# A gate's condition blocks multiplied and added by GpSimd instead of VectorE

## The chip, the cores and the metric

One core of one Trainium2 chip runs the whole kernel in one launch. The metric is the device time of one execution in microseconds (us). Engines are named as the profile names them: PE is TensorE (matmuls), PEld its weight loads, DVE is VectorE, ACT is ScalarE, POOL is GpSimd, SP is SyncE. Each engine works through its own queue in order.

## The reference

A trunk of four layers over 512 tokens of width 1024, in float32. Each layer has a token mixer (latent attention, stick-breaking attention, retention, latent attention) and a dense MLP. Each half layer is normed, shifted and scaled ahead of the mixer or MLP, and gated behind it, by vectors that come from one condition vector:

```
cond = silu(c)                                   # (1, 1024)
mod = cond @ ada_w[i] + ada_b[i]                 # (1, 6144), for layer i
sh_a, sc_a, g_a, sh_f, sc_f, g_f = split(mod, 6)
h = rms_norm(x, norm_g[i, 0]) * (1 + sc_a) + sh_a
x = x + g_a * rms_norm(mixer(h), norm_g[i, 1])
h = rms_norm(x, norm_g[i, 2]) * (1 + sc_f) + sh_f
x = x + g_f * rms_norm(mlp(h), norm_g[i, 3])
```

The latent attention of layers 0 and 3 has 8 heads with a causal softmax over 512 keys. The change touches `g_a` of layer 0, the gate that is applied to the attention's output.

## The kernel before, in words

Float32 products on PE are made of three passes over a high and a low part of each operand (`mm3`, lines 91 to 93); `split` (lines 85 and 86) makes the parts, the high one on ACT, the low one on DVE. Tokens are worked in four blocks of 128.

**The condition products.** A vector such as `g_a` is 1024 columns of `cond @ ada_w`. The first shift and scale are made at the start (`ada_start`); all others are made by the generator `ada`, beside other work. Its rows are cut into eight blocks of 128 rows, 512 KB each. For a block, `load` issues a DMA in POOL's queue (line 301) into a raw tile 128x1024, of which there are three. DVE then multiplies the tile by the block's 128 condition values, one per partition (line 313, the first block, into the accumulator `adaacc`), or multiplies and adds to the accumulator in one instruction (line 315, the seven others). So partition p of `adaacc` holds the sum of eight rows, and what is left is a sum over partitions: `columns_of` does that by DVE transposes of 32x32 (line 338), DVE sums (line 341), a matmul with a folding matrix (line 348) and small additions. A call of `next(bg)` makes one block, or one step of `columns_of`. A load is issued two blocks ahead, and waits for its raw tile to be free.

**The work around it.** During layer 0's attention `bg` is `ada` with the gate's job first (blocks 0 to 7) and then shift and scale of the MLP half (blocks 8 to 23). The attention is a pipeline over heads; at each step t the program text has, in this order:

```
order = ((B, 0), (C1, 1), (C2, 2), (A, -2), (B2, 0))   # stage, lag
for stage, lag in order:
    if 0 <= t - lag < n:
        stage(t - lag)
if t >= 0:
    for _ in range(3):
        next(bg, None)
```

`A` makes k, q and, for every fourth head, v of a head (PE, with copies on ACT and DVE; lines 751 to 758 rotate q). `B` is `softmax_rows`: the scores on PE; on DVE a mask and a row maximum per query block (line 884); on POOL one instruction on a 128x4 tile that turns the maxima into biases (line 887); on ACT the exponentials with their sums (line 889). `B2` takes reciprocals of the sums on DVE (line 783) and normalises on ACT (line 785). `C1` transposes the probabilities on PE (line 903) and splits them, `C2` multiplies with v. The banks of PSUM that these stages use are shared, four for the scores and four for all else.

**Who sets the order.** A planner puts every engine's instructions into a queue ahead of time: it plays the program through with its own durations, and each engine takes, of what is ready, what stands first in the program text. `held` and `after` add order without a wait. The queues are then fixed. At the start of the kernel (lines shown as L1305) instructions go strictly in the text's order.

Later stages (the attention's output projection, where the gate is first used, the MLP and the other layers) follow in PE's queue.

Of the kernel before, what the change touches and what calls it, by code (L numbers as in the profile page):

```python
# [12 lines left out]
ALU = mybir.AluOpType  # L13

P = 128
S = 512
# [27 lines left out]
class Trunk:  # L44
# [239 lines left out]
            pass  # L284
        yield

    def ada(self, jobs):

        nc = self.nc
        blocks = [(job, i, kb) for job in jobs for i in range(len(job[2])) for kb in range(KB)]
        raws, due, sums = {}, [], {}

        def load(n):
            if n < len(blocks):
                (l, part, names), i, kb = blocks[n]
                col = (3 * part + self.ROWS[names[i]]) * D
                raws[n] = self.adap.tile([P, D], F32, tag="araw", name="adaraw", bufs=AHEAD + 1)  # L300
                self.after(nc.gpsimd.dma_start(out=raws[n], in_=self.d_ada_w[l][kb * P:kb * P + P, col:col + D]), self.mm)  # L301

        for n in range(AHEAD):
            load(n)
        for n, (job, i, kb) in enumerate(blocks):
            load(n + AHEAD)
            if due and next(due[0], self) is self:
                due.pop(0)
            rv = raws.pop(n)
            wcol = self.cond[:, kb:kb + 1]  # L310
            if kb == 0:
                a = self.adap.tile([P, D], F32, tag="acc", name="adaacc", bufs=1)
                ins = nc.vector.tensor_scalar(a, rv, wcol, None, ALU.mult)
            else:
                ins = nc.vector.scalar_tensor_tensor(a, rv, wcol, a, ALU.mult, ALU.add)  # L315
            self.held(ins)
            if kb == KB - 1:
                due.append(self.columns_of(job, i, a, sums))
            yield
        while due:  # L320
            if next(due[0], self) is self:
                due.pop(0)
            else:
                yield
# [892 lines left out]
    def run(self, ctx):  # L1217
        nc = self.nc
        mixers = self.mixers
        kinds = {"mla": self.mla, "sb": self.sb, "ret": self.ret}  # L1220
        none = lambda: None
        tables = {"mla": (lambda: list(self.mla_tables()), self.mla_tables_T), "sb": (none, none), "ret": (self.ret_tables, none)}
        self.xn, self.mods, self.gates = {}, {}, {}
        self.hold = self.late = None
        phases = []
        seen = {}
        bg = self.ada([(0, 0, ("G",)), (0, 1, ("sh", "S"))])
        for l, kind in enumerate(mixers):
            j = seen[kind] = seen.get(kind, -1) + 1
            m, f = Phase(l, 0), Phase(l, 1)  # L1230
            wanted = [(0, 1, ("G",))] if l == 0 else []
            if l + 1 < len(mixers):
                wanted += [(l + 1, p, ("sh", "S", "G")) for p in (0, 1)]
                t = tables[mixers[l + 1]]
            else:
                t = (none, none)
            m.gen = lambda nxt, k=kinds[kind], j=j, m=m, bg=bg: k(j, m, nxt, bg)
            f.gen = lambda nxt, l=l, f=f, bg=self.ada(wanted), t=t: self.ffn(l, f, nxt, bg, t)
            bg = iter(())
            phases += [m, f]  # L1240
        for a, b in zip(phases, phases[1:] + [None]):
            a.nxt = b
        first, mod = phases[0], (0, 0)
        self.starting, self.h_pool = True, True
        setup = self.setup(ctx)
        next(setup)
        halves = [self.ada_start([(n, half) for n in ("S", "sh")]) for half in (0, 1)]
        rope = self.mla_tables()
        next(halves[0])
        for _ in setup:  # L1250
            pass
        next(rope)
        for _ in range(X0 - 1):
            next(halves[0])
        self.load_x()
        next(halves[0])
        next(rope)
        rs = [self.x_rstd(tb) for tb in range(TB)]
        for tb in range(TB):
            self.pre_norm(tb, rs[tb])  # L1260
        next(rope)
        for _ in range(7 - X0):
            next(halves[0])
        first.go()
        for _ in halves[0]:
            pass
        for _ in rope:
            pass
        for _ in range(ST0):
            next(halves[1])  # L1270
        for g in (0, 1):
            for kb in (0, 2):
                self.turn(g, mod, kb, kb + 2)
                for _ in range(ST1):
                    next(halves[1], None)
        for _ in range(8 - ST0 - 4 * ST1):
            next(halves[1])
        first.go()
        for _ in halves[1]:
            pass  # L1280
        first.go()
        self.h_pool = False
        for g in (0, 1):
            self.turn(g, mod, 4, 8)
        tables[mixers[0]][1]()
        self.starting = False
        for p in phases:
            p.finish()
# [94 lines left out]
```

## Time and profile before

| what | value |
|---|---|
| median of 3 runs | 2502.9 us (2502.72 to 2504.25) |
| the profiled execution's own time | 2503.81 us |
| its span in the trace | 2502.0 us |
| mean granted clock of PE | 0.991 |
| PE busy | 2418.3 us, 97% |
| DVE busy | 1544.3 us, 62% |
| ACT busy | 1089.1 us, 44% |
| POOL busy | 248.5 us, 10% |
| layer 0's attention heads (about) | 84 to 180 us |
| the gate's eight blocks on DVE | 94.2 to 112.3 us |

The span is what lies between the first and the last instruction in the trace; the execution's time is 1.8 us longer. Busy shares are of the whole span: what an engine's time is worth in one stage is read from that stage.

### The profile page before, as it was taken

Reading aid. Unit: us, or ns where it says so; the run is one execution under the profiler, and the core shown is the slowest. Engines: PE = TensorE matmul, PEld = TensorE weight load, DVE = VectorE, ACT = ScalarE, POOL = GpSimd, SP = SyncE. Lnnn points to the kernel's source line nnn. Section 1 sums busy time; section 2 is a strip of 40 time slices with the busy share of each in tenths; the row PEclk is TensorE's granted clock in tenths of the full one; section 3 lists DMA queues with packets and bytes.
Section 4 is the critical chain, followed back from the end, with each engine's and each line's share of the span. In section 5 each row is a group of like instructions: output and inputs, shape, how many; then the busy total and the mean of one; then the engine's idle time right before and its main releaser. Section 6 shows DMA issues by size and latency. Waiting matters only on the chain.

```text
span 2502.0 us, 30936 instructions
## 1 busy us (share of the span) xinstructions
PE 2418.3 (97%) x11733; PEld 2027.1 (81%) x11733; DVE 1544.3 (62%) x2333; ACT 1089.1 (44%) x2002; POOL 248.5 (10%) x495
## 2 busy tenths in 40 slices
PE   5889999999998999999999999999999999999998
PEld 4778888888886888888788888888888778888886
DVE  6896666666888567765644444476665676633443
ACT  6665332235665533323533334453233576632331
POOL 5311100101000110000100000100010310000000
PEclk9999999999999999999999999999999999999999
DMA  7354765743210475663322232365663303333331
GB/s 237 99 177 137 236 200 173 219 144 125 64 35 25 153 236 157 210 200 99 128 76 92 80 103 85 112 219 166 210 209 95 96 18 127 96 99 101 94 95 48
DMA packets 204534, 329.95 MB, mean 132 GB/s; under 512 B 15968, under 2 KB 115168, under 8 KB 204384
## 3 DMA queue, kind: packets, MB, share of 16 engines
q1 hardware_dynamic: 179040, 235.69, 29.9%
q0 software_dynamic: 25344, 92.29, 11.5%
q8 instruction: 92, 1.51, 0.2%
q14 instruction: 58, 0.48, 0.1%
HBM read 319.51 MB, written 8.42 MB: 131 GB/s over the span
## 4 chain that ended last, share of the span: by engine, by line
PE 84%; DVE 6%; ACT 5%; issue 3%; POOL 2%; DMA 1%; SPq 0%; POOLq 0%; DVEq 0%; ACTq 0%
PE acc L93 15%; PE acc L92 15%; PE acc L91 15%; PE mmp L91 13%; PE mmp L92 13%; PE mmp L93 13%; ACT probs L889 1%; ACT junk L136 1%; POOL rstd L131 1%; PE trp L903 1%; DVE u L1029 1%; POOL var L128 1%; DVE x L439 0%; DVE b L1030 0%; ACT probs L785 0%
## 5 line engine op out<-in xcount | busy, mean ns | idle before, releaser
L86 DVE TENSOR_TENSOR wl<-raw,wh 128x1024 fp32r<-128x1024 f32 (+1 forms) x356 | 434.5, 1223 | 422.6 <-ACT wh L85 420.1
L85 ACT CAST wh<-raw 128x1024 fp32r<-128x1024 f32 (+1 forms) x356 | 373.7, 1051 | 656.0 <-PE acc L93 369.3
L92 PE MATMUL mmp<-hl,wh 128*128 128x512 f32 (+1 forms) x1408 | 520.8, 371 | 2.4 <-DVE hl L86 2.4
L93 PE MATMUL mmp<-hh,wl 128*128 128x512 f32 (+1 forms) x1408 | 519.7, 370 | 0.0
L91 PE MATMUL mmp<-hh,wh 128*128 128x512 f32 (+1 forms) x1408 | 518.5, 372 | 1.0 <-DVE ol L86 0.9
L91 PE MATMUL acc<-wh,h1h 128*128 128x512 f32 x1024 | 399.2, 390 | 0.0
L93 PE MATMUL acc<-wh,h1l 128*128 128x512 f32 x1024 | 398.5, 389 | 0.0
L92 PE MATMUL acc<-wl,h1h 128*128 128x512 f32 x1024 | 398.5, 389 | 0.0
L92 PEld LDWEIGHTS mmp<-hl,wh 128*128 128x128 f32 x1408 | 265.3, 188 | 48.3 <-DVE hl L86 3.9
L93 PEld LDWEIGHTS mmp<-hh,wl 128*128 128x128 f32 x1408 | 265.3, 188 | 45.0
L91 PEld LDWEIGHTS mmp<-hh,wh 128*128 128x128 f32 x1408 | 263.5, 188 | 47.2 <-DVE ol L86 2.0
L93 PEld LDWEIGHTS acc<-wh,h1l 128*128 128x128 f32 x1024 | 192.2, 188 | 39.9
L92 PEld LDWEIGHTS acc<-wl,h1h 128*128 128x128 f32 x1024 | 192.3, 188 | 39.8
L91 PEld LDWEIGHTS acc<-wh,h1h 128*128 128x128 f32 x1024 | 192.2, 188 | 39.9
L315 DVE SCALAR_TENSOR_TENSOR adaacc<-adaraw,cond,adaacc 128x1024 f32<-128x1024 f32 x154 | 197.1, 1280 | 6.0 <-DMA adaraw<-in_ada_w_dram 5.4
L301 POOL DMA_DIRECT2D adaraw<-in_ada_w_dram x176 | 94.1, 535 | 749.4 <-DVE adaacc L315 428.9
L85 ACT CAST h1h<-relu 128x512 fp32r<-128x512 f32 (+1 forms) x144 | 81.8, 574 | 143.0 <-DVE relu L529 143.0
L528 ACT ACTIVATE relu<-mmp 128x512 f32<-128x512 f32 (+1 forms) x144 | 77.9, 547 | 123.4 <-PE mmp L93 123.1
L93 PE MATMUL acc<-wh,hl 128*128 128x512 f32 (+1 forms) x320 | 123.8, 390 | 5.6 <-DVE hl L86 4.3
L529 DVE TENSOR_TENSOR relu<-mmp,relu 128x512 f32<-128x512 f32 (+1 forms) x144 | 89.7, 627 | 62.5 <-ACT relu L528 62.4
L91 PE MATMUL acc<-wh,hh 128*128 128x512 f32 (+1 forms) x320 | 124.2, 391 | 4.1 <-ACT hh L1305 3.8
L86 DVE TENSOR_TENSOR h1l<-relu,h1h 128x512 fp32r<-128x512 f32 (+1 forms) x144 | 90.2, 631 | 59.9 <-ACT h1h L85 59.9
(309 smaller groups left out, 3603.8 us busy)
## 6 DMA issues: line engine op xcount, KB each, us to landing
raw<-in_ffn_w_dram SPq DMA_DIRECT2D x256, 512.0 KB, 3.8
adaraw<-in_ada_w_dram POOLq DMA_DIRECT2D x176, 512.0 KB, 4.8
raw<-in_ret_w_in_dram SPq DMA_DIRECT2D x48, 512.0 KB, 4.0
raw<-in_sb_w_in_dram SPq DMA_DIRECT2D x24, 512.0 KB, 3.8
x<-x SPq DMA_DIRECT2D x48, 256.0 KB, 3.6
adaw<-in_ada_w_dram SPq DMA_DIRECT2D x32, 256.0 KB, 5.3
raw<-in_mla_w_out_dram SPq DMA_DIRECT2D x16, 512.0 KB, 4.5
raw<-in_ret_w_out_dram SPq DMA_DIRECT2D x16, 512.0 KB, 4.4
```

Of the source, the lines that this page charges most:

```text
L85: ins = self.nc.scalar.copy(hi, src)
L86: (engine or self.nc.vector).tensor_sub(lo, src, hi.bitcast(F32))
L91: first = self.mm = mm(ps, l[0], r[0], start=start, stop=False)
L92: mm(ps, l[0], r[1], start=False, stop=False)
L93: mm(ps, l[1], r[0], start=False, stop=stop)
L128: self.nc.gpsimd.tensor_scalar(v, ss, ss2, EPS, ALU.add, ALU.add)
L131: self.last = self.nc.gpsimd.tensor_tensor(r, v, self.mhalf[:, 0:w], ALU.pow)
L136: self.nc.scalar.activation(junk[:, 0:src.shape[-1]], src, AF.Square, scale=scale, accum_out=acc_out)
L301: self.after(nc.gpsimd.dma_start(out=raws[n], in_=self.d_ada_w[l][kb * P:kb * P + P, col:col + D]), self.mm)
L315: ins = nc.vector.scalar_tensor_tensor(a, rv, wcol, a, ALU.mult, ALU.add)
L528: nc.scalar.activation(r, ps, AF.Relu)
L529: nc.vector.tensor_mul(r, ps, r)
```

## The change

The eight blocks of layer 0's first gate go from DVE to POOL. [...] So one multiply and seven multiply-adds on DVE become eight multiplies and seven additions on POOL. Loads, transposes and everything behind them stay on their engines, and all other jobs keep DVE. The POOL instructions aren't `held`.

```
-    def ada(self, jobs):
+    def ada(self, jobs, pool_job=None):
...
             wcol = self.cond[:, kb:kb + 1]
             if kb == 0:
                 a = self.adap.tile([P, D], F32, tag="acc", name="adaacc", bufs=1)
-                ins = nc.vector.tensor_scalar(a, rv, wcol, None, ALU.mult)
+            if job == pool_job:
+                t = a if kb == 0 else rv
+                nc.gpsimd.tensor_scalar(t, rv, wcol, None, ALU.mult)
+                if kb:
+                    nc.gpsimd.tensor_tensor(a, a, rv, ALU.add)
+            elif kb == 0:
+                self.held(nc.vector.tensor_scalar(a, rv, wcol, None, ALU.mult))
             else:
-                ins = nc.vector.scalar_tensor_tensor(a, rv, wcol, a, ALU.mult, ALU.add)
-            self.held(ins)
+                self.held(nc.vector.scalar_tensor_tensor(a, rv, wcol, a, ALU.mult, ALU.add))
...
-        bg = self.ada([(0, 0, ("G",)), (0, 1, ("sh", "S"))])
+        bg = self.ada([(0, 0, ("G",)), (0, 1, ("sh", "S"))], (0, 0, ("G",)))
```

## Rows read from the trace of the kernel before

**Rows 1.** The page: busy us, share of span, instructions of each engine.
```profile
PE 2418.3 (97%) x11733; PEld 2027.1 (81%) x11733; DVE 1544.3 (62%) x2333; ACT 1089.1 (44%) x2002; POOL 248.5 (10%) x495
```

**Rows 2.** By stretches: length, busy PE, PEld, DVE, ACT, POOL; PE clock; DMA.
```profile
100.00:120.00 20.00, 16.27 (x78) 13.45 (x77) 16.75 (x31) 14.33 (x35) 2.95 (x6) 0.91 0.54 171
120.00:140.00 20.00, 18.16 (x99) 15.38 (x98) 19.44 (x44) 11.59 (x32) 3.10 (x7) 0.91 0.33 94
...
180.00:200.00 20.00, 20.00 (x102) 16.63 (x101) 14.78 (x23) 9.43 (x14) 0.00 (x0) 1.00 0.58 187
```

**Rows 3.** Chain of waits, 84 to 130 us: start, length, who.
```profile
89.06 2.30 ACT probs L889 x8
...
94.32 0.67 DVE adaacc L313
...
97.30 4.91 DMA adaraw<-in_ada_w_dram
...
102.30 1.29 DVE adaacc L315
...
104.70 0.40 ACT probs L785
```

**Rows 4.** Timeline of PE: start, length, instruction, idle before and releaser.
```profile
105.15 0.33 PE L903 MATMUL trp<-ident,probs 128*128 128x128 f32 x1 [3.11 <-ACT probs L785]
...
121.55 1.25 PE L903 MATMUL trp<-ident,probs 128*128 128x128 f32 x10
```

**Rows 5.** DVE's instructions by groups, 93 to 125 us.
```profile
L315 DVE SCALAR_TENSOR_TENSOR adaacc<-adaraw,cond,adaacc 128x1024 f32<-128x1024 f32 x7 | 9.0, 1281 | 1.6 <-DMA adaraw<-in_ada_w_dram 1.5
```

**Rows 6.** Timeline of ACT and DVE between 98 and 123 us.
```profile
98.92 0.40 ACT L889 ACTIVATE probs<-probs,max 128x128 f32<-128x128 f32 x1 [2.76 <-POOL max L887]
...
109.73 2.60 DVE L315 SCALAR_TENSOR_TENSOR adaacc<-adaraw,cond,adaacc 128x1024 f32<-128x1024 f32 x2
...
113.61 1.64 ACT L785 ACTIVATE probs<-probs,rz 128x256 f32<-128x256 f32 x3
...
122.51 0.70 DVE L338 STREAM_TRANSPOSE aT<-adaacc 128x512 f32<-128x512 f32 x1
```

**Rows 7.** Timeline of POOL at the start of the kernel.
```profile
1.14 0.29 POOL masks.py:199 TENSOR_SCALAR_AFFINE_SELECT ident<-ident 128x128 f32<-128x128 f32 x1
...
18.28 0.30 POOL L1305 TENSOR_SCALAR var<-ssx 128x1 f32<-128x1 f32 x1 [0.41 <-ACT junk L1305]
...
26.49 0.83 POOL L1305 TENSOR_TENSOR ropet<-ropet 128x128 f32<-128x128 f32 x1 [5.25 <-ACT ropet L1305]
...
29.04 0.55 POOL L1305 TENSOR_SCALAR snk<-ropek 128x128 f32<-128x128 f32 x1
...
36.20 1.18 POOL L1305 TENSOR_TENSOR hl<-ht,hh 128x256 fp32r<-128x256 f32 x1
...
58.20 0.19 POOL L130 TENSOR_SCALAR var<-ssq 128x1 f32<-128x1 f32 x1 [3.18 <-ACT junk L136]
```

**Rows 8.** Timeline of DVE and POOL where the two run at once.
```profile
26.31 0.75 DVE L1305 SCALAR_TENSOR_TENSOR adaacc<-adaw,cond,adaacc 128x512 f32<-128x512 f32 x1 [0.41 <-DMA adaw<-in_ada_w_dram]
...
35.69 2.24 DVE L1305 SCALAR_TENSOR_TENSOR adaacc<-adaw,cond,adaacc 128x512 f32<-128x512 f32 x2
...
163.06 1.28 DVE L315 SCALAR_TENSOR_TENSOR adaacc<-adaraw,cond,adaacc 128x1024 f32<-128x1024 f32 x1
...
163.34 1.09 POOL L887 TENSOR_SCALAR max<-max 128x4 f32<-128x4 f32 x1 [1.00 <-DVE max L884]
```

**Rows 9.** Timeline of POOL, 84 to 140 us.
```profile
87.87 1.85 POOL L301 DMA_DIRECT2D adaraw<-in_ada_w_dram  x3
...
97.30 0.54 POOL L301 DMA_DIRECT2D adaraw<-in_ada_w_dram  x1 [1.48 <-DVE adaacc L315]
97.91 0.98 POOL L887 TENSOR_SCALAR max<-max 128x4 f32<-128x4 f32 x1
...
108.70 0.21 POOL L887 TENSOR_SCALAR max<-max 128x4 f32<-128x4 f32 x1 [4.29 <-DVE max L884]
```

## The prediction

> **What bounds the kernel now.** I read the page first. TensorE (PE) is busy 97% of the span, GpSimd (POOL) 10% [rows 1]; over the whole kernel VectorE (DVE) is no bound. Such shares are averages, so I next read the table by stretches around the place of the change. Between 180 and 200 us PE is busy in all of its 20 us: from there on a microsecond lost earlier shifts everything behind it. Between 100 and 120 us, in the attention of layer 0, it is busy only 16.27 us, its granted clock is 0.91, and DVE is busy 16.75 us; from 120 to 140 DVE is busy 19.44 us [rows 2]. So the edit falls into one of the few stretches where PE isn't the limit, and DVE is close to it.
>
> The chain of waits shows how. DVE takes its queue in order. The first condition block's multiply (94.32) stands there among head 1's softmax maxima; a later block (102.30) waits for its load, issued at 97.30, and everything behind it in the queue waits too, the reciprocal of head 1's sums among it, so that ScalarE (ACT) starts head 1's normalisation only at 104.70 [rows 3]. PE waits 3.11 us for that before its transposes at 105.15 [rows 4].
>
> **What is removed.** Of the eight gate blocks, one multiply and seven multiply-adds of 1.281 us [rows 5]; with some 0.7 for the multiply (0.67 of it in the chain [rows 3]) that is 0.7 + 7 x 1.28 = 9.7 us of DVE, between 94.3 and 109.73 + 2.60 = 112.3 us [rows 3, 6], and DVE's wait for the load. The trace shows what it can give at most: PE's wait of 3.11 us, and the lower clock, 9% of 20 us or 1.8 us, if PE no longer stops. That is about 5 us [rows 2, 4]. The rest of the 9.7 us lies beside PE work.
>
> **What is added.** Eight multiplies and seven additions of 128x1024 in POOL's queue. The trace has none of that size, so I bound them.
>
> Multiply: four strips of 32 columns, 128x128 in all, took 0.55 us with DVE idle, and one of 128x1 0.19 [rows 7]. (0.55 - 0.19)/127 is 2.8 ns a column, which makes 0.19 + 1023 x 2.8 = 3.1 us for 1024: the upper end. A contiguous 128x128 (the diagonal select) took 0.29: 0.8 ns a column, 1.0 us: the lower end. The moved operands are contiguous, so I take the lower slope, with 0.1 to 0.2 for the per-partition factor (a 128x1 with one took 0.30 against 0.19 [rows 7]): 1.2 us.
>
> Addition: the 128x128 product that began at 26.49 ended at 27.32, and the subtraction of 128x256 that began at 36.20 ended at 37.38 [rows 7]. Both stood behind a DVE multiply-add with two SBUF inputs: the first DVE instruction ran from 26.31 to 27.06, the second from 35.69; two of these DVE instructions together took 2.24 us where alone one takes 0.75 [rows 8]. Measured from the end of the DVE instruction (27.06, and 36.79 if the first took 1.10 of the 2.24) POOL needed 0.26 and 0.59 us: 2.6 ns a column between them. 0.59 + 768 x 2.6 gives 2.6; the proportion from 256 columns, 4 x 0.59, gives 2.4; the product's own 4 x 2 x 0.26 gives 2.1. I take 2.3. Ends: 1.4 (if of the 256 columns only 0.36 us, the time by which the DVE instruction was stretched from 0.75, belong to the stream: 4 x 0.36) and 4.7 (4 x the whole 1.18).
>
> Each block also issues a load in POOL's queue, 0.54 to 0.6 us as now [rows 9]; gaps between POOL instructions are near 0.08 (97.30 + 0.54 to 97.91). A block is thus 1.2 + 2.3 + 0.16 + 0.6 = 4.3 us (ends 3.2 and 8.6), where DVE took 1.28; the job is 8 x 1.2 + 7 x 2.3 and some 6 for issues and gaps, 32 us against 18 us on DVE now.
>
> The Trainium skill speaks against such a move: "GPSIMD Engine Reference", section "Performance versus the Vector engine", gives an addition of 2048 fp32 columns 4.5 us on GpSimd, about twice VectorE's, while an operation with one input runs near line rate. By it, halved, an addition would take an estimated 2.25 us, and the sum would stay as it is; no row of this trace has an addition that wide.
>
> **What stands behind it in the queue.** POOL also scales the softmax maxima of each head (line 887), and ACT's exponentials wait for that. The program text has the three blocks of step t ahead of the maxima of head t + 1, and the order of the loads now (the one at 97.30, which waits for block 1, stands ahead of head 1's scaling at 97.91 [rows 9]) says that the planner keeps that. So I lay POOL's queue out. The first loads are issued from 87.87 [rows 9] and land, as the load in the chain with 4.91 us [rows 3], at about 92.7.
>
> - Block 0: 92.7 + 1.2 + issue 0.6 = 94.5. Blocks 1 and 2: 94.5 + 2 x 3.66 + one issue 0.6 = 102.4. Head 1's maxima are scaled at 102.5 to 102.7; now that ends at 98.89 [rows 9]. The exponentials begin 3.9 us later than their 98.92 [rows 6] and take 2.3, as head 0's [rows 3]; reciprocal and normalisation follow at about 105.4 against 104.70, since the wait on DVE is gone: +0.7.
> - Blocks 3 to 5: 102.7 + 3 x 4.3 = 115.6. Head 2's maxima are late by 6.9 us (now 108.70 [rows 9]). Their cover: head 2 is normalised by 113.61 + 1.64 = 115.25, and PE turns it at 121.55 [rows 4, 6]: 6.3 us. Left over: 0.6. If that cover is gone, because ACT's queue keeps its present order and the copies that free PE's banks stand behind the late exponentials, it costs up to the whole 6.9.
> - Blocks 6 and 7: 115.8 + 2 x 4.3 = 124.4. DVE's transposes of the gate's sum start at 122.51 now [rows 6]: 1.9 us late on a path shifted by about 1; what is late next is the DVE work queued behind them, head 3's maxima. About +0.9. After this POOL is as before.
>
> PE's waiting falls in part: with head 1's exponentials late, the planner, which orders the engines' queues by its own estimate, can put the work that is ready, head 0's copies and its product with V, ahead of them, and PE then isn't idle for 3.11 us. I count half, -1.2 net of the clock staying as it is.
>
> Sum: 0.7 + 0.6 + 0.9 - 1.2 = +1.0 us. Against the profiled execution's 2503.81 that is 2504.8. That execution is 0.9 above the median of the three runs, so on the median: 2503.9. With half a microsecond for the port, below, I forecast 2504.5: no change to be told. About 0.2% of this kernel, 5 us, is what a measurement can tell from none.
>
> **The rivals.**
>
> *POOL's queue is the bound (slower).* At 3.1 us a multiply a block takes 6.2: head 1's maxima at 92.7 + 3.7 + 2 x 5.56 + 0.6 = 108.1, head 2's at 108.3 + 18.6 = 126.9, or 18.2 late, less 6.3 of cover: about +12, and 2515. For it: the only multiplies undisturbed by DVE are those strips. Against it: their rows of 32 columns. At 1.2 us a multiply the same happens if ACT's order stays as it is: +6.9 - 0.5, 2509. It decides when head 2's maxima are over 11 us late, or when the cover isn't used.
>
> *The shared port (slower).* POOL's scaling of 128x4 took 0.21 at 108.70, but 1.09 at 163.34, ending just after the DVE multiply-add that began at 163.06 [rows 8, 9]; above, DVE was stretched in turn. With POOL busy most of 30 us, the DVE instructions with two SBUF inputs in the stretch wait for it: one of line 753 and two of line 758, at most 2.3 us each, on the way from q to the scores: at most +7, 2510. The other DVE instructions there read PSUM for one input, and the strongest contenders, the multiply-adds themselves, are gone. I count 0.6 of it. The Trainium skill has this as a rule ("SBUF — State Buffer", section "Who interferes with whom"): a VectorE instruction with two SBUF inputs and a GpSimd instruction that reads SBUF exclude each other for the whole instruction; by that rule, the trace agrees.
>
> *DVE's relief shows (faster).* If the planner puts head 1's scaling ahead of the blocks, exponentials begin once the four maxima are taken (now interleaved with two blocks, 1.9 us less), the reciprocal no longer waits for a load, and PE loses neither the 3.11 us nor the 1.8 of clock: -5 to -6, 2497. For it: the loads' arrival may leave POOL free when the maxima come. Against it: the order in the program text, and that head 2's maxima, ready soon after, meet the same queue.
>
> *Nothing comes of it* can't be in the strict sense, the work does move; it is the forecast itself that it cancels out.
>
> **Numbers.** Forecast, with its own range of 2499 to 2508: 0.47. Queue: 0.27. Port: 0.08. Relief: 0.18. The first is "same", the next two "slower" (0.35), the last "faster". For eight in ten I leave out the lowest part of the relief and, above, the queue with dear multiplies and dear additions together (8.6 a block gives +25): 2496.5 to 2517.
>
> **What would show it.** Multiplies of about 1.2 and additions of about 2.3 us on POOL; DVE 9.7 us less busy; head 1's scaling near 102.6, head 2's near 115.6, the gate's transposes near 124.4; PE between 100 and 120 us busy within a microsecond or two of its 16.27. Wrong it would be if the strips' slope holds, if ACT waits for head 2's scaling with PE idle behind it, or if the scalings come ahead of the blocks.

## The result and the profile after

The changed kernel took 2521.45 us (median of 4 runs, 2520.41 to 2525.14) beside 2503.02 for the kernel before, run beside it: a ratio of 1.0073, 95% interval 1.006 to 1.0085. It is 18.4 us slower, outside the range forecast (2496.5 to 2517). The profiled execution took 2522.23 us, with a span of 2520.4.

The page shows little of it: PE's busy time is that of [rows 1] within 4 us, and POOL's grew by 38.5 us.

```profile
PE 2422.2 (96%) x11733; PEld 2031.8 (81%) x11733; DVE 1538.6 (61%) x2325; ACT 1090.3 (43%) x2002; POOL 287.0 (11%) x510
```

The table by stretches (columns as in [rows 2]) shows where. From 100 to 140 us PE is busy 23.0 us, not 34.4, at a mean granted clock of 0.74, not 0.91; DVE is busy 15.8, not 36.2; POOL is busy nearly without a break. DVE was relieved, and then waited.

```profile
100.00:120.00 20.00, 11.81 (x56) 9.97 (x55) 6.01 (x16) 7.32 (x18) 19.71 (x11) 0.74 0.33 100
120.00:140.00 20.00, 11.21 (x53) 9.76 (x52) 9.81 (x15) 8.71 (x21) 19.04 (x12) 0.74 0.15 42
140.00:160.00 20.00, 17.15 (x87) 15.04 (x86) 16.22 (x36) 10.31 (x29) 3.22 (x7) 0.83 0.52 169
```

POOL's timeline (answering to [rows 9]; lines of the file have moved by some five: L315 is now the multiply, L317 the addition, L892 the scaling of the maxima) shows the queue. Between one scaling and the next stand three blocks of a multiply of 2.84, a load's issue of 0.6 and an addition of 2.4 us.

```profile
88.81 0.23 POOL L892 TENSOR_SCALAR max<-max 128x4 f32<-128x4 f32 x1 [2.07 <-DVE max L889]
89.10 1.85 POOL L301 DMA_DIRECT2D adaraw<-in_ada_w_dram  x3
...
102.40 2.84 POOL L315 TENSOR_SCALAR adaraw<-adaraw,cond 128x1024 f32<-128x1024 f32 x1
105.20 0.61 POOL L301 DMA_DIRECT2D adaraw<-in_ada_w_dram  x1
105.84 2.35 POOL L317 TENSOR_TENSOR adaacc<-adaacc,adaraw 128x1024 f32<-128x1024 f32 x1
108.28 0.22 POOL L892 TENSOR_SCALAR max<-max 128x4 f32<-128x4 f32 x1
...
126.10 0.22 POOL L892 TENSOR_SCALAR max<-max 128x4 f32<-128x4 f32 x1
...
144.26 0.22 POOL L892 TENSOR_SCALAR max<-max 128x4 f32<-128x4 f32 x1 [4.85 <-DVE max L889]
```

The chain of waits says that this queue sets the end: from 93.44 to 137.73 us it never leaves POOL, and behind the gate's sum it goes over a load that POOL could issue only then.

```profile
93.44 3.18 POOL adaacc L315
...
108.28 0.22 POOL max L892
...
126.10 0.22 POOL max L892
...
135.42 2.31 POOL adaacc L317
137.73 4.15 DMA adaraw<-in_ada_w_dram
...
141.98 0.75 DVE adaacc L319
```

Who waits is seen on DVE's and PE's timelines (idle time before, and its releaser, in brackets). DVE takes its queue in order, and the reciprocal of a head's sums stands in it ahead of the next head's maxima, which were ready (the first row), and of the differences and the split of q that the next head's scores need (the second and third). These differences also read copies that ACT makes, and in ACT's queue the copies stand behind the late exponentials (the row of ACT at 128.54). PE waits 8.19 and 8.79 us for all this, where it waited 3.11 [rows 4].

```profile
110.85 0.18 DVE L788 RECIPROCAL rz<-sum 128x4 f32<-128x4 f32 x1 [9.40 <-ACT probs L894]
...
128.67 0.18 DVE L788 RECIPROCAL rz<-sum 128x4 f32<-128x4 f32 x1 [6.41 <-ACT probs L894]
129.18 3.44 DVE L763 TENSOR_TENSOR qpe<-qpe,qpe 64x512 fp32r<-64x512 f32 x2 [0.33 <-ACT qpe L762]
...
141.98 0.75 DVE L319 TENSOR_SCALAR adaacc<-adaraw,cond 128x1024 f32<-128x1024 f32 x1 [2.65 <-DMA adaraw<-in_ada_w_dram]
```

```profile
128.54 1.24 ACT L762 CAST qpe<-qpe 64x512 fp32r<-64x512 f32 x2
```

```profile
111.36 0.45 PE L91 MATMUL acc<-knh,qnh 128*128 128x128 f32 x1 [8.19 <-DVE max L889]
...
133.39 0.79 PE L91 MATMUL mmp<-wh,lath 128*128 128x512 f32 x1 [8.79 <-DVE qnl L86]
...
144.82 0.80 PE L91 MATMUL mmp<-lath,wh 128*128 128x512 f32 x1 [2.55 <-DVE pTl L86]
```

Nearly all of the loss is there by 144 us. Head 0's scaling began at 88.81 against 87.59 in the trace of the kernel before, so 1.2 us of the difference arose ahead of the change. From the end of head 0's scaling to that of head 1's it is 19.5 us (before: 11.1), to head 2's another 17.8 (10.0), to head 3's start 17.9 (17.4): 8.4 + 7.8 + 0.6 = 16.8 us, and with the 1.2 that is 18.0 of the 18.4 in the spans. (Head 4's scaling, at 156.72 against 137.07, is 19.6 late; 1.2 of that come back behind it.)

### The profile page after: what moved, and what is told of

Read it like the earlier page. It is cut to its first block, busy times and chain, and to the rows that moved or that the text cites. A ratio compares the mean times of both kernels' runs of the same rounds, so it can differ in the third digit from the quotient of the medians.

```text
span 2520.4 us, 30927 instructions
## 1 busy us (share of the span) xinstructions
PE 2422.2 (96%) x11733; PEld 2031.8 (81%) x11733; DVE 1538.6 (61%) x2325; ACT 1090.3 (43%) x2002; POOL 287.0 (11%) x510
## 4 chain that ended last, share of the span: by engine, by line
PE 83%; DVE 6%; ACT 4%; POOL 3%; issue 2%; DMA 1%; SPq 0%; POOLq 0%; DVEq 0%; ACTq 0%
PE acc L92 14%; PE acc L93 14%; PE acc L91 14%; PE mmp L91 12%; PE mmp L92 12%; PE mmp L93 12%; ACT junk L136 1%; POOL adaraw L315 1%; POOL rstd L131 1%; ACT probs L894 1%; POOL adaacc L317 1%; PE trp L908 1%; DVE u L1034 1%; POOL var L128 1%; DVE x L444 0%
## 5 line engine op out<-in xcount | busy, mean ns | idle before, releaser
L321 DVE SCALAR_TENSOR_TENSOR adaacc<-adaraw,cond,adaacc 128x1024 f32<-128x1024 f32 x147 | 188.0, 1279 | 5.5 <-DMA adaraw<-in_ada_w_dram 5.0
L128 POOL TENSOR_SCALAR var<-ssy 128x1 f32<-128x1 f32 x32 | 18.7, 583 | 955.0 <-ACT junk L136 955.0
```

The source lines that it names most:

```text
L128: self.nc.gpsimd.tensor_scalar(v, ss, ss2, EPS, ALU.add, ALU.add)
L321: self.held(nc.vector.scalar_tensor_tensor(a, rv, wcol, a, ALU.mult, ALU.add))
```

## The experiments

The theory: POOL's queue is the bound, because a multiply costs 2.84 us and not 1.2. The rivals: the port that POOL shares with DVE; the one wait for the scaling, with the rest of the queue harmless; the new order in which the planner puts the other engines' instructions. "Head 2's lateness" below is the time from head 0's to head 2's scaling, less the 21.1 us of the kernel before (87.59 to 108.70).

The versions ran on several chips, each beside runs of the kernel before, whose medians went from 2503.0 to 2504.6. The ratios below, and the losses in us, are against these. A difference of two versions can be taken between their medians or between their losses, and the two can be up to 1.6 us apart; both are given where it matters.

**m0_prices**: a kernel of its own, without the trunk, in which POOL does these operations on 128 partitions, alone and beside DVE.

> GpSimd's instructions by themselves, without the trunk (the output is only the input copied): multiplies with a per-partition factor, additions, a multiply by a constant, a copy, four strips of 32 columns, first with VectorE idle, then beside VectorE instructions with two SBUF inputs, then beside VectorE instructions that read PSUM. Queue theory: a contiguous multiply of 128x1024 takes 2.8 us and an addition 2.4 us with VectorE idle already. Port theory: with VectorE idle the multiply takes about 1.2 us and only beside two-input instructions 2.8 us or more.

Its groups of instructions (after the bar: busy us of the group, mean ns of one); in the first two rows POOL's multiplies and DVE's multiply-adds of two SBUF operands run at once, in the others DVE is idle:

```profile
L114 DVE SCALAR_TENSOR_TENSOR dvetwo<-a,b 128x1024 f32<-128x1024 f32 x12 | 24.2, 2013 | 0.4
...
L83 POOL TENSOR_SCALAR beside2mulptr<-a 128x1024 f32<-128x1024 f32 x2 | 7.2, 3579 | 0.1
...
L83 POOL TENSOR_SCALAR alonemulptr<-a 128x1024 f32<-128x1024 f32 x2 | 5.7, 2842 | 0.2
...
L87 POOL TENSOR_TENSOR aloneadd<-a,b 128x1024 f32<-128x1024 f32 x2 | 4.7, 2337 | 0.2
L94 POOL TENSOR_TENSOR mulbc<-a 128x1024 f32<-128x1024 f32 x2 | 3.8, 1892 | 0.1
...
L97 POOL COPY copy<-a 128x1024 f32<-128x1024 f32 x2 | 2.1, 1038 | 0.1
```

A multiply by a factor for each partition is 0.60 us for 128 columns and 2.84 for 1024, 2.5 ns a column; four strips of 32 columns take the same 0.60 as 128 in a row. The part meant for DVE instructions that read PSUM ran for the most part beside the last two-operand ones; only the first two of its 20 fell beside POOL's last addition, and they kept their 0.69 us.

**e_scale_dve, e_scale_act, b_scale_act**: only the scaling is taken out of POOL's queue, in layer 0; the third does so in the kernel before. The planner then orders the other engines' queues anew as well.

```
-        nc.gpsimd.tensor_scalar(m, m, -MLA_SCALE, None, ALU.mult)
+        if self.layer0: nc.scalar.activation(m, m, AF.Copy, scale=-MLA_SCALE)   # e_scale_dve: nc.vector.tensor_scalar
+        else:           nc.gpsimd.tensor_scalar(m, m, -MLA_SCALE, None, ALU.mult)
```

> The changed kernel, with layer 0's maxima scaled by VectorE instead of GpSimd. If the whole loss is the scalings' place behind the blocks, it goes: 2503 to 2508 us. Queue theory in full: GpSimd still ends the gate's sum near 137 us, and VectorE's queue has the gate's transposes ahead of head 3's maxima, near 122 us, so the wait moves there: PE's two waits of 8 us go, one of 10 to 15 us comes, 2514 to 2520 us. If the port or the new order of the queues made the loss, it stays near 2521 us with no such single wait.

> The changed kernel, with layer 0's maxima scaled by ScalarE (neither GpSimd's queue nor the port it shares with VectorE). Queue theory: the gate's sum still ends near 134 us and VectorE waits for it ahead of head 3's maxima, so this is no better than with the scaling on VectorE: 2511 to 2515 us. If the scalings that VectorE held up at the port (2.8 and 3.5 us instead of 0.16) made that version's loss: 2504 to 2508 us.

> The kernel before, with layer 0's maxima scaled by ScalarE, as a control for the other edits. Three of the eight scalings took 1.0 to 1.1 us on GpSimd instead of 0.2, and each has a hop from VectorE to GpSimd to ScalarE: 0 to 4 us faster, 2499 to 2504 us.

Measured: 2514.41 us (ratio 1.0046, 1.0029 to 1.0063), 2516.51 (1.0052, 1.0038 to 1.0065) and 2502.84 (0.9997, 0.9988 to 1.0006). Without the scaling in POOL's queue the kernel is 5 to 7 us faster (6 to 8 by the losses); e_scale_act is 1.5 us above its range. What is left has moved to the gate's sum, for which DVE now waits 12 us with head 3's maxima behind it (first row, e_scale_act). On DVE the scaling itself was held up beside POOL: 3.53 us, and 0.16 once POOL was idle (the other rows, e_scale_dve).

```profile
135.49 1.30 DVE L343 STREAM_TRANSPOSE aT<-adaacc 128x512 f32<-128x512 f32 x2 [12.02 <-POOL adaacc L317]
```

```profile
108.79 3.53 DVE L893 TENSOR_SCALAR max<-max 128x4 f32<-128x4 f32 x1
...
138.68 0.16 DVE L893 TENSOR_SCALAR max<-max 128x4 f32<-128x4 f32 x1
```

**e_three, e_half, e_mulbc**: a shorter queue in three ways: three blocks on POOL; all eight over half the columns, which leaves out the other half of the gate's sum and so shows a time only; a product with the broadcast factor for the multiply.

```
e_three: if job == pool_job and kb < 3:
e_half:  nc.gpsimd.tensor_scalar(t[:, 0:512], rv[:, 0:512], wcol, None, ALU.mult)    # and the addition likewise
e_mulbc: nc.gpsimd.tensor_tensor(t, rv, wcol.broadcast_to([P, D]), ALU.mult)
```

> The changed kernel, with only the first three blocks on GpSimd and five on VectorE. Queue theory: head 1's scaling stays near 107 to 108 us, head 2's is late only by what head 1 lost, and the gate's sum is in time: about a third to a half of the loss, 2508 to 2512 us. If what costs is the end of the sum and the late loads, no loss: 2502 to 2505 us.

> The changed kernel, with GpSimd's multiplies and additions on 512 of the 1024 columns (the other half of the gate's sum is left out; VectorE clears the accumulator once, 0.5 us). Queue theory: a block costs about 1.5 + 1.25 + 0.75 = 3.5 us, head 1's scaling comes near 102 us, head 2's near 113, the sum ends near 121: a loss of 0 to 5 us, 2503 to 2508 us, far less than half of 18. A loss in proportion to GpSimd's work, as by the port: 2510 to 2513 us. A loss by the order alone: 2515 us or more.

> The changed kernel, with GpSimd's multiply written as a product of two tensors, the factor broadcast along the row (1.89 us for 128x1024 by itself, against 2.84). Queue theory: 0.95 us less a block: head 1's scaling 2.8 us earlier, head 2's 5.7, the end of the sum 7.6 us, and the time follows the queue: 2513 to 2516 us. If the queues' new order or the number of instructions makes the loss, it stays within 2 us of 2521.

Measured: 2509.6 (1.0027, 1.0016 to 1.0038), 2506.09 (1.0011, 1.0002 to 1.002), 2513.83 (1.0041, 1.0027 to 1.0055). e_mulbc changes nothing but the multiply's price: PE, DVE and ACT have the same instructions in the same order in its trace and in the change's. 8 x 0.95 = 7.6 us less queue made the kernel 7.6 us faster (8.5 by the losses), and no new order can have done that. With head 2's lateness of 3.8 (e_half), 5.7 (e_three), 10.8 (e_mulbc) and 16.2 us (the change), the loss was 2.0, 5.5, 9.9 and 18.4 us.

**e_loads_sp**: the next job's loads leave POOL's queue.

```
-  nc.gpsimd.dma_start(out=raws[n], ...)
+  (nc.sync if pool_job and n >= 8 else nc.gpsimd).dma_start(out=raws[n], ...)
```

> The change's kernel, but the loads of the blocks from the ninth on (the next job's, which GpSimd issued at 137.73 us behind its last addition) are issued from SyncE's queue. If the wait of VectorE for that load (2.65 us, a load of 4.15 us in the chain behind the gate's sum) is a term of the loss, the time falls by 1.5 to 3 us, to 2518.5 to 2520, and head 3's scaling, at 144.26 us, comes that much earlier. Rival (the late sum alone sets head 3's maxima, the load is beside it): 2521 to 2522, with the scaling at 144 still.

Measured: 2516.56 (1.0049, 1.0035 to 1.0063), 4.9 us below the change (6.5 by the losses), more than expected; PE's order is the change's. DVE's wait of 2.65 us is gone, and with it a slow clock: in the change PE, having waited 2.55 us, went through nine matmuls from 144.82 to 148.83, one start every 0.43 us or so, at a granted clock of 0.50, the level of 1.2 GHz; here, at a granted clock of 1.00, the same nine took from 143.34 to 145.44, one every 0.23. That is 1.9 us; 2.65 + 1.9 = 4.55, near the 4.5 between the two spans. In the rows it is the distance of the starts that counts, as one matmul's length reaches into the next.

```profile
146.27 0.63 PE L91 MATMUL mmp<-lath,wh 128*128 128x512 f32 x1
146.69 0.63 PE L92 MATMUL mmp<-latl,wh 128*128 128x512 f32 x1
```

```profile
144.08 0.39 PE L91 MATMUL mmp<-lath,wh 128*128 128x512 f32 x1
144.30 0.39 PE L92 MATMUL mmp<-latl,wh 128*128 128x512 f32 x1
```

**e_mul_dve**: DVE multiplies, POOL adds.

```
-                nc.gpsimd.tensor_scalar(t, rv, wcol, None, ALU.mult)
+                self.held(nc.vector.tensor_scalar(t, rv, wcol, None, ALU.mult))
```

> Half of the change: VectorE multiplies the eight gate blocks (about 0.7 us each as in the kernel before), GpSimd only adds (2.34 us) and issues. A block then takes some 3.1 us of GpSimd's queue instead of 5.95. Theory (time follows GpSimd's queue): head 1's scaling near 102, head 2's near 110, the sum's end near 116: 2502 to 2508. Rival (the price of the port: each of VectorE's multiplies, with one SBUF input, is held beside GpSimd's additions as its scalings of 128x4 were, to 2.3 to 3.5 us): 2509 to 2515, with multiplies of over 2 us in the trace.

Measured: 2505.73 (1.0005, 0.9996 to 1.0014), the same as before, head 2's lateness 3.9 us. Both expectations were half right: the time is in the range that the queue gives, and yet DVE's multiplies, 0.75 us alone, took 1.85 on average beside the additions, 13.8 us for the eight, where the blocks had taken 9.7 in all before.

```profile
L315 DVE TENSOR_SCALAR adaraw<-adaraw,cond 128x1024 f32<-128x1024 f32 x7 | 13.0, 1854 | 0.0
L315 DVE TENSOR_SCALAR adaacc<-adaraw,cond 128x1024 f32<-128x1024 f32 x1 | 0.8, 750 | 0.0
```

**e_spread, e_defer**: the cheaper product and ACT's scaling together, and the sum made less urgent: by 1.5 blocks a head instead of three (e_spread), or by a buffer of its own for the gate's sum, turned seven blocks later (e_defer).

```
e_spread: if job == pool_job: yield            # a second one behind each block
e_defer:  a = (self.rowp.tile([P, D], F32, tag="G") if job == pool_job else self.adap.tile([P, D], F32, tag="acc", bufs=1))
          later = (n + 7, self.columns_of(job, i, a, sums))
```

> The changed kernel with three edits: the cheaper multiply, the scaling on ScalarE, and a step's pause behind each of the gate's blocks, so that 1.5 of them fall to a step instead of 3 and the planner puts the gate's transposes behind head 6's maxima instead of ahead of head 3's. Queue theory: nobody waits for GpSimd any more, the sum ends near 133 us and is wanted later; VectorE is rid of 9.7 us in heads 1 to 3 but gets the next job's blocks crowded at the end: 2499 to 2506 us. If GpSimd's work costs as such, by the port: 2508 us or more.

> The change's kernel with three edits that take away whoever waits for GpSimd: the multiply is a product with the broadcast factor (1.89 us in the price run, not 2.84), ScalarE scales layer 0's maxima, and the gate's sum has its own buffer and is turned seven blocks later, behind a later head's maxima. GpSimd's chain of blocks then ends near 131 to 133 us with nobody due before it. Theory (GpSimd's queue in the way is the whole loss): the time comes back to the kernel before's, or gains the wait of 3.1 us that stood there for the load: 2499 to 2506. Rival (what remains is the shared port: VectorE's multiply-adds of the next job and its two products at head 2 now run beside GpSimd's all along and slow each other): 2507 or more, with multiply-adds of clearly more than 1.28 us between 100 and 131 us and with GpSimd's product above 1.89.

Measured: 2507.26 (1.001, 1.0001 to 1.0019) and 2511.62 (1.003, 1.0019 to 1.004). The first lies between the two times that were expected. In e_spread the attention itself is faster than before (PE busy 36.4 us of the 40 from 100 to 140, against 34.4), but the next job's blocks now come at the layer's end, and PE is busy only 13.80 of the 20 us from 200 to 220, which were full before: it waits 7.46 us there for the next job's sum. In e_defer, where nobody is due for POOL's results, the time is in the port's range, though not by the multiply-adds that the expectation names. Two differences of 64x512, 1.40 us the pair alone, took 8.87, the first alone 4.12 (DVE, then POOL, then PE behind them):

```profile
113.97 8.87 DVE L771 TENSOR_TENSOR qpe<-qpe,qpe 64x512 fp32r<-64x512 f32 x2 [0.69 <-ACT qpe L770]
...
113.97 4.12 DVE L771 TENSOR_TENSOR qpe<-qpe,qpe 64x512 fp32r<-64x512 f32 x1 [0.69 <-ACT qpe L770]
```

```profile
113.29 2.39 POOL L320 TENSOR_TENSOR adaacc<-adaacc,adaraw 128x1024 f32<-128x1024 f32 x1
115.63 1.90 POOL L318 TENSOR_TENSOR adaraw<-adaraw,cond 128x1024 f32<-128x1024 f32 x1
117.46 0.60 POOL L301 DMA_DIRECT2D adaraw<-in_ada_w_dram  x1
118.09 2.35 POOL L320 TENSOR_TENSOR adaacc<-adaacc,adaraw 128x1024 f32<-128x1024 f32 x1
120.39 1.89 POOL L318 TENSOR_TENSOR adaraw<-adaraw,cond 128x1024 f32<-128x1024 f32 x1
122.22 0.60 POOL L301 DMA_DIRECT2D adaraw<-in_ada_w_dram  x1
```

```profile
123.62 0.79 PE L91 MATMUL mmp<-wh,lath 128*128 128x512 f32 x1 [8.37 <-DVE qnl L86]
```

**e_defer_psum, a_psum, b_psum**: e_defer, the change and the kernel before, each with the rotated part of q kept in PSUM in layer 0, so that the differences and the sum ahead of them read one operand from SBUF.

```
+                t2 = ps2                                   # the second product in place, in PSUM
                 nc.vector.tensor_mul(t2, ps2, self.sn)
-                nc.vector.tensor_add(t1, t1, t2)
+                nc.vector.tensor_add(ps1, t1, t2); t1 = ps1
```

> The kernel of e_defer, in which nobody waits for GpSimd's results, with one more edit: in layer 0 the rotated part of q is kept in PSUM (second product, sum and the source of the two differences), so that these VectorE instructions read one operand from SBUF and not two. Port theory: there the two differences, which took 8.87 us beside GpSimd's chain and 1.40 alone, take 1.4 again, TensorE's wait of 8.4 us for them goes, and the time falls by 6 to 8.5 us, to 2503 to 2506. Rival (the wait belongs to something else in GpSimd's queue, or one SBUF operand is enough to be shut out): 2510 to 2512, with the differences still at 3 us or more each.

> The change's kernel with the same PSUM edit alone: what the port is worth inside the change. The differences took 2.21 and 3.44 us there against 1.40; head 2's pair stands in front of the scores behind which GpSimd's sum is awaited anyway. Theory (GpSimd's queue sets the time, the port's delays lie beside it): 2519 to 2522. Rival (the port's delays add to the queue's): lower by their sum of 2.8 us or more, 2518 or less.

> Control: the kernel before with the same PSUM edit. GpSimd is idle there while the differences run (1.40 us the pair), so all theories expect no difference beyond what longer-held PSUM banks cost: 2502 to 2506.

Measured: 2509.7 (1.0023, 1.0013 to 1.0033), 2525.13 (1.0085, 1.0071 to 1.0098), 2508.36 (1.0019, 1.001 to 1.0028). The control missed: the edit itself costs 4.6 us. The loss is there before POOL's first block: in b_psum the first loads are issued at 93.0, not 87.9, and in a_psum head 0's scaling is at 92.31, not 88.81. The differences took 0.69 us each in all three. a_psum too is above both of its ranges, and e_defer_psum lies between its two. If the edit's cost adds, the port was worth 1.9 + 4.6 = 6.5 us in e_defer (5.6 by the losses; the stall was 7.5), and 4.6 - 3.7 = 0.9 us in the change (1.7 by the losses), no more than these medians can tell from nothing. That the cost adds is not shown.

**e_mul_dve_act**: e_mul_dve with the PSUM edit and ACT's scaling.

> The kernel of e_mul_dve (VectorE multiplies, GpSimd adds) with the PSUM edit and with layer 0's scaling on ScalarE: GpSimd then holds up neither the exponentials nor the differences, only the gate's sum, which ended at 119.3 us in e_mul_dve, before the transposes are due at 122.5. If queue and port are the whole loss, VectorE's relief (1.28 us a block down to about 0.75) is left over: 2499 to 2503, faster than the kernel before. Rival (VectorE's relief is worth nothing here, since what it gives back lies beside TensorE's work or is given to VectorE's waits for GpSimd's additions to free the buffers): 2503 to 2506.

Measured: 2512.51 (1.0033, 1.002 to 1.0045). That is above both ranges, and even less the 4.6 us of the PSUM edit it is no faster than e_mul_dve; the multiplies again took 1.56 us, not 0.75. No version with blocks on POOL beat the kernel before.

## Why the prediction was wrong

The failed step is the price of the multiply. The text had both ends, "the upper end" of 3.1 us from the strips and "the lower end" of 1.0 from the diagonal select, and took 1.2 because "the moved operands are contiguous". It measured 2.84 in the trace and 2.84 alone. Strips and contiguous columns cost the same (0.60 for 128x128); the select was simply another operation. The trace of the kernel before had a row that says so, an operation of the right kind on contiguous columns, if beside DVE's multiply-adds:

```profile
27.41 0.61 POOL L1305 TENSOR_SCALAR ropek<-ropet 128x128 f32<-128x128 f32 x1
```

A block then is 2.84 + 2.4 + 0.6 + gaps, 5.9 us and not 4.3. With the prediction's own cover that price gives its rival's 2515, still inside the range; the two next terms that were wrong, the cover and the loads behind the gate's sum, took the time out of it.

- **Addition, load, order.** 2.3 forecast, 2.34 to 2.43 measured, 2.73 beside a difference of DVE; 0.6 as forecast; three blocks ahead of each scaling, as laid out. The 2.3 was in part luck: it rests on 0.26 and 0.59 us for 128 and 256 columns, which take 0.45 and 0.72 alone; the slope between them was too steep (2.6 ns a column, measured 2.1), and the errors cancel. The Trainium skill ("GPSIMD Engine Reference", section "Performance versus the Vector engine") has 4.5 us for an addition of 2048 columns; the estimate halved from it, 2.25, agrees with 2.34. What the same page says in its section "Engine selection", that one input is roughly line rate, does not hold for this operation: the multiply with a factor for each partition (2.84) was dearer than the addition, and only the copy (1.04) was cheap.
- **The scalings.** Forecast 102.5 and 115.6, measured 108.28 and 126.10. The rival "POOL's queue is the bound" had 108.1 and 126.9, and was given 0.27. It reads right up to here.
- **The cover.** Forecast and rival both counted 6.3 us at head 2, read at PE's transposes [rows 4, 6]. But the path to head 3 doesn't go over those: in DVE's queue head 2's reciprocal stands ahead of the differences of q for head 3, and in ACT's queue the copies that these read stand behind the exponentials, so late exponentials hold up the next head's scores. From head 2's scaling to head 3's the kernel before takes 17.56 us; of the versions that leave the scaling on POOL the shortest are 15.42 (e_loads_sp), 15.48 (e_mul_dve) and 15.50 (e_half). The cover that any of them used is 2.1 us. The text named this case ("if that cover is gone, because ACT's queue keeps its present order") and priced it only with cheap multiplies.
- **The gate's sum and what follows.** Forecast at 124.4, measured at 137.73. That POOL issues the next job's loads behind all its blocks was in no term, neither the forecast's nor the rival's; e_loads_sp puts it at 4.9 us (6.5 by the losses), with the clock. The rival's 2515 with 4.2 us less cover and these 4.9, less 2.0 because head 2 was 16.2 and not 18.2 us late, makes 2522, close to the 2521.45 measured; but that sum was made afterwards, and its terms need not add.
- **DVE's relief.** Forecast at -1.2, as a rival at -6. It came to nothing: DVE then waited 9.40 and 6.41 us for the late exponentials of heads 1 and 2, and its busy time fell by 5.7 us and not by 9.7. With half of the change (e_mul_dve) the time was the same, and there DVE's multiplies beside POOL took 13.8 us, more than the 9.7 removed.
- **The port.** Counted at 0.5; 0.9 to 1.7, or nothing, in the change. DVE's delays there (3.44 us for 1.40) lie in stretches that POOL's queue sets anyway. In e_defer, without that queue in the way, it is the largest term, if the PSUM edit's cost adds.

The loss is shown to follow POOL's queue (e_mulbc: 7.6 to 8.5 us for 7.6, in an unchanged order) and to divide between scaling, sum and loads (e_scale_act, e_loads_sp). The division isn't additive, and the port's share in the change rests on the PSUM edit's cost adding.

## What to carry to other kernels

Price a moved operation by the same operation with the same kind of operands, look for its row in the trace before taking another's, and where two rows disagree by a factor of three, carry the dear one through the whole layout. Before blocks go into an engine's queue, list everything else that this queue issues, the small scalings and next loads too, and when each is due. Measure cover on the path to the next bottleneck, through the queue order of each engine on it, not at the nearest idle consumer.

## What the runs showed of the hardware

On GpSimd a 128x1024 multiply with a factor for each partition took 2.84 us and by a constant 2.77, but a two-operand product with the factor broadcast 1.89, an addition 2.34, a copy 1.04.

In e_defer a VectorE instruction that needed the shared port waited over two GpSimd instructions: the first difference waited through the rest of an addition and all of the product that followed at once, the second did the same, and each of the two ended within 0.03 us of the end of a load's issue (118.09 beside 118.06, 122.84 beside 122.82). That isn't so everywhere. In the change the second difference of the pair at 129.18 got in between an addition and a multiply that followed at once: the pair ended at 132.62, and the multiply took 3.29 us and not 2.84. What decides is not shown.

```profile
129.33 2.73 POOL L317 TENSOR_TENSOR adaacc<-adaacc,adaraw 128x1024 f32<-128x1024 f32 x1
132.04 3.29 POOL L315 TENSOR_SCALAR adaraw<-adaraw,cond 128x1024 f32<-128x1024 f32 x1
```

The Trainium skill ("SBUF — State Buffer", section "Who interferes with whom") has whoever issues first hold the port for the whole instruction. For additions the traces agree that the two exclude each other, and e_defer shows a wait over two instructions; for a multiply they do not quite agree: in the change a pair of differences that began at 93.22 had ended by 95.43, inside a multiply that ran from 93.44 to 96.62 (the profile's spans on GpSimd are rough).

```profile
93.22 2.21 DVE L763 TENSOR_TENSOR qpe<-qpe,qpe 64x512 fp32r<-64x512 f32 x2 [0.43 <-ACT qpe L762]
...
93.44 3.18 POOL L315 TENSOR_SCALAR adaacc<-adaraw,cond 128x1024 f32<-128x1024 f32 x1 [2.49 <-DMA adaraw<-in_ada_w_dram]
```

VectorE instructions with one SBUF operand and a factor were held too (0.16 us became 3.53, 0.75 up to 3.22); the same section counts `tensor_scalar` among those that can take the shared port. Those that read PSUM for one operand (0.69 us) were not held.
